# A hybrid streaming encoder layer: first projection in the order value, query, key, value, with queries and keys turned by VectorE

## The chip, the cores and the metric

The kernel runs on one core of one Trainium2 chip. The metric is the device time of one execution in microseconds (us). TensorE (PE) does the matrix products, VectorE (DVE), ScalarE (ACT) and GpSimd (POOL) the rest; SyncE (SP) issues nearly all DMA transfers.

## The reference

One layer of a streaming encoder for 384 tokens: 256 of a new prompt, and 16 for each of 8 running streams. `h` is projected by one matrix into a gated convolution input, queries, keys, values, forget logits and two gates:

```python
h = rmsnorm(x, norm_mix_g)                      # (384, 2048)
proj = h @ w_in                                 # columns: GLU 2048 | q 1024 | k 1024 | v 1024 | f 8 | gates 2 x 2048
q = rmsnorm(q, q_norm_g); k = rmsnorm(k, k_norm_g)          # per head of 128
logf = log_sigmoid(f_logit + b_forget)
b_out = attn_fn(q, k, v, logf) @ w_att_out      # 8 heads, causal, bias from cumsum(logf)
x = x + (gate_a * a_out + gate_b * b_out) @ w_out           # a_out: conv branch
x = x + (silu(gc) * u_half) @ w_down            # ConvGLU feed-forward, width 5632
```

Normalized keys, the values, `logf` and two convolution states are outputs too.

## The kernel before

Everything is float32. Each matrix product is done as three products of rounded halves: a weight pair (256 rows by up to 512 columns) is loaded into a `raw` tile (three buffers), ACT casts it to `hi` (line 145), DVE subtracts to get `lo` (line 146; `hi` and `lo` have three buffers each), and TensorE runs `hi*hi`, `hi*lo` and `lo*hi` for each 128-row tile (lines 239 to 241 where the weights are stationary, 244 to 246 where the activations are). `plan` lists the weight pairs in the order of their use, and `ahead` fetches and splits two or three pairs ahead at a raised priority. `gemm` walks over jobs: 16 row blocks of 128 ("units"), then the eviction of the PSUM tiles; after each unit `tick` advances side work (generators, and functions put off with `after(units, fn)`). TensorE's order is the program's; the orders of DVE, ACT and of the SP queue come from a scheduler that works with those priorities. Each of these queues is in order.

The first stage projects `h` by token rows (three 128-token tiles, so three PSUM tiles a job; five `acc` banks and three `misc` banks rotate):

- values and forget logits in three blocks of 344 columns, `V_COLS`; the first two share a pass over `h`, since in it `x` is still being loaded, turned by TensorE and scaled (`x_chunk`). In the same pass `first_norm` collects the sums of squares; its last steps make the row factor `rs1` (ACT square root, line 111, then DVE), which every eviction of this stage multiplies in (`tok_evac`, lines 426 and 428);
- keys, two blocks of 512, with `bias_rows` at their side, then the key norm on DVE (lines 519 and 520) and the key store;
- queries, two blocks of 512, and the query norm (line 528).

The gated unit follows (four jobs with stationary weights, lines 239 to 241, 16 units each). Beside it runs attention, one head each six units: `head_past_keys`, `head_operands` two units later, `head_scores` two after that. `head_operands` turns the head's queries and keys from token rows to feature rows: three TensorE transposes of `qt` (line 583) and an ACT copy that scales (584), three of `kt` (587) and a DVE copy (588), then a DVE copy of the streams' queries into the padded `qz` (589).

In the mixing stage and the feed-forward the kernel already turns 512-column panels on DVE: `blocks` (line 259) makes 16 block transposes of 32 partitions by 384, of which each turns twelve 32x32 blocks, and puts them where a full transpose would.

Of the kernel before, what the change touches and what calls it, by code (L numbers as in the profile page):

```python
# [15 lines left out]
P = 128  # L16
# [24 lines left out]
def hybrid_step(  # L41
# [31 lines left out]
    def misc_tile():  # L73
        return misc.tile([P, 512], F32, tag="misc", name="misc")
# [97 lines left out]
    FFN_PLAN += [("up", g) for g in range(7, 9)] + [("down", (6, 7))]  # L172
    FFN_PLAN += [("up", g) for g in range(9, 11)] + [("down", (8, 9, 10))]

    planned(w_in, 0, V_COLS[0], 16, V_COLS[1])
    for cols in V_COLS[2:] + K_COLS + Q_COLS + GLU_COLS + GA_COLS + GB_COLS:
        planned(w_in, 0, cols, 16)
    AO_PW = [("ao", 0), ("ao", 1), ("pw", 0), ("ao", 2), ("pw", 1), ("ao", 3), ("pw", 2), ("pw", 3)]
    for what, n in AO_PW:
# [41 lines left out]
    def gemm(jobs, sides=()):  # L221
        for js in jobs:
            js = js if isinstance(js, tuple) else (js,)
            for j in js:
                nb = 4 if j["kind"] == "A" else NTT
                j["ps"] = [(misc_tile if j is not js[0] and i == 2 else acc_tile)() for i in range(nb)]
            for j, k in [(j, k + i) for k in range(0, js[0]["nk"], 2) for j in js for i in range(2)]:
                nb, n, nk, ps = len(j["ps"]), j["n"], j["nk"], j["ps"]
                kk = k % 2
                if kk == 0:  # L230
                    ahead(2 if len(plan) > v_last + 3 else 3)
                    hi, lo = ready.pop(0)
                ah, al = j["act"](k)
                st, sp = k == 0, k == nk - 1
                for m in range(nb):
                    s = slice(m * P, (m + 1) * P)
                    if j["kind"] == "A":
                        o = ps[m][:, :NT]
                        mm(o, hi[:, kk, s], ah, start=st, stop=False)  # L239
                        mm(o, hi[:, kk, s], al, start=False, stop=False)  # L240
                        mm(o, lo[:, kk, s], ah, start=False, stop=sp)  # L241
                    else:
                        o = ps[m][:, :n]
                        mm(o, ah[:, s], hi[:, kk, :n], start=st, stop=False)  # L244
                        mm(o, ah[:, s], lo[:, kk, :n], start=False, stop=False)  # L245
                        mm(o, al[:, s], hi[:, kk, :n], start=False, stop=sp)  # L246
# [141 lines left out]
    def first_norm():  # L388
        for c in range(2, 16, 2):
            if c == 2:  # L390
                yield
            yield
            x_chunk(c)
            yield
            x_chunk(c + 1)
            if c % 4 == 2:
                for t in range(NTT):
                    n = c // 4
                    tc.keep_in_program_order(
                        nc.scalar.activation(junk[:], xs[n][:, t, :], AF.Square, accum_out=ssx[:, t, n:n + 1]))  # L400
# [7 lines left out]
        nc.vector.tensor_copy(rs1[:], r[:])  # L408
# [27 lines left out]

    ha = grouped(hT)
    v_jobs = [job("B", 16, ha, tok_evac(vt, 344 * i, 344, shared=i == 2), n=344) for i in range(3)]
    gemm([(v_jobs[0], v_jobs[1]), v_jobs[2]], [first_norm()])
    close_x0()  # L440


    def tiny(name):
# [21 lines left out]
    nc.sync.dma_start(prompt_v[0, 0].rearrange("(t p) h d -> p t (h d)", p=P), vt[:, 0:2, 0:1024])  # L465
    nc.sync.dma_start(sample_v[0].rearrange("b t h d -> (b t) (h d)"), vt[:, 2, 0:1024])

    p_dr, close_dr = pool("dram", space=bass.MemoryType.DRAM)
    p_b, close_b = pool("bias", side="right")
# [41 lines left out]
        ts(ssf, ssf, 1.0 / P, EPS, op0=ALU.mult, op1=ALU.add)  # L511
        return rsqrt(ssf, [P, NTT * H], p_qkv, f"rq{a}")[:].rearrange("p (t h) -> p t h", t=NTT)

    gemm([job("B", 16, ha, tok_evac(kt, 512 * i, 512, 0)) for i in range(2)], [bias_rows()])
    close_b()
    rk = head_rsqrt(0)
    for t in range(NTT):
        k3 = kt[:, t, :].rearrange("p (h d) -> p h d", h=H)
# [6 lines left out]
    rq = head_rsqrt(1)  # L525
    for t in range(NTT):
        q3 = qt[:, t, :].rearrange("p (h d) -> p h d", h=H)
        tt(q3, q3, rq[:, t, :].unsqueeze(2).to_broadcast([P, H, P]), op=ALU.mult)


    p_att, close_att = pool("att", side="right")
# [42 lines left out]
            load_k(d["h"] + 1)  # L574

    def head_operands(d):
        hs = d["hs"]
        d["vc"], d["bs"] = vbs[d["h"]]
        qT = p_att.tile([P, NT], F32, tag="qT", bufs=2, name="qT")
        kT = p_att.tile([P, NT], F32, tag="kT", bufs=2, name="kT")  # L580
        ps = misc_tile()
        for t in range(NTT):
            tr(ps[:, t * P:(t + 1) * P], qt[:, t, hs], ident[:])
        nc.scalar.activation(qT[:], ps[:, :NT], AF.Identity, scale=qgs[:])
        ps = misc_tile()
        for t in range(NTT):
            tr(ps[:, t * P:(t + 1) * P], kt[:, t, hs], ident[:])
        nc.vector.tensor_copy(kT[:], ps[:, :NT])
        nc.vector.tensor_copy(qz[d["h"] % 2][:, :, :, 0:16], by_stream(qT[:, 2 * P:]))
        d["qT"], d["kT"] = qT, kT  # L590

    def head_scores(d):
        qT, kT, kTs, bs, qzh = d["qT"], d["kT"], d["kTs"], d["bs"], qz[d["h"] % 2]
        s0 = misc_tile()
        mm(s0[:, :P], qT[:, 0:P], kT[:, 0:P], start=True, stop=True)
        s1 = misc_tile()
        mm(s1[:, :2 * P], qT[:, P:2 * P], kT[:, 0:2 * P], start=True, stop=True)
        s2_ = misc_tile()
        mm(s2_[:, P:2 * P], qT[:, 2 * P:], kT[:, 2 * P:], start=True, stop=True)
# [51 lines left out]
    def attention():  # L651
        at = {}
        for d in heads:
            for off, step in ((0, head_past_keys), (2, head_operands), (4, head_scores), (9, head_probs),
                              (11, head_out), (13, head_last)):
# [426 lines left out]
```

## Time and profile before

| | us |
|---|---|
| median of three runs | 2008.67 |
| the runs | 2007.51, 2008.67, 2492.07 |
| the profiled execution | 2007.84 |
| its span in the profile | 2005.8 |

The profile is of one execution. Its page gives the busy time of each engine, the chain of work that ended last, and groups of equal instructions by line; the trace behind it can be asked for who waited for whom and for single instructions. A line such as `60.52 0.32 PE L244 MATMUL acc<-hi,hT ...` gives start and duration in us, engine, source line, operation, the tile written and those read. In brackets stands the idle time of the engine before it and what ended it. The ends of matmuls are modelled and overlap; their starts are what counts.

### The profile page before, as it was taken

What the parts mean: (1) busy time and instruction counts of PE and PEld (TensorE: products, weight loads), DVE (VectorE), ACT (ScalarE), POOL (GpSimd) and SP (SyncE); (2) the same over time, 40 slices, a digit from 0 to 9 for tenths busy, and PEclk for the clock granted to TensorE, in tenths of its full rate; (3) what the DMA queues carried; (4) which work ended last, traced back from release to release, by engine and by line L of the source; (5) the groups of instructions that cost most, each with busy time, mean ns of one, the idle gap of its engine ahead of it and who ended that gap; (6) DMA issues with size and microseconds to landing.
All of it is one profiled execution on the core that took longest, in us unless ns stands there. A gap on an engine that the chain in (4) does not pass through costs nothing.

```text
span 2005.8 us, 24525 instructions
## 1 busy us (share of the span) xinstructions
PE 1995.2 (99%) x9458; PEld 1682.9 (84%) x9458; DVE 1269.1 (63%) x1854; ACT 744.2 (37%) x1085; POOL 87.1 (4%) x214
## 2 busy tenths in 40 slices
PE   9999999999999999999999999999999999999999
PEld 8988999988888888888888888888888888888887
DVE  4434478888765487576767683367673376638663
ACT  5434454433334523333333432233332233323321
POOL 2000001100000000000000010000010000000000
PEclk9999999999999999999999999999999999999999
DMA  6566467444444334534444434444443444344443
GB/s 185 171 176 176 138 155 174 121 134 131 138 130 126 126 124 146 178 124 128 124 131 125 137 122 137 131 127 124 129 137 126 129 124 137 127 127 126 137 156 107
DMA packets 200574, 275.99 MB, mean 138 GB/s; under 512 B 45022, under 2 KB 88049, under 8 KB 200449
## 3 DMA queue, kind: packets, MB, share of 16 engines
q1 hardware_dynamic: 200137, 273.85, 46.0%
q8 instruction: 74, 1.21, 0.2%
q0 software_dynamic: 288, 0.57, 0.2%
q14 instruction: 43, 0.35, 0.1%
q10 hardware_dynamic: 32, 0.01, 0.0%
HBM read 266.98 MB, written 7.86 MB: 137 GB/s over the span
## 4 chain that ended last, share of the span: by engine, by line
PE 95%; DVE 4%; issue 1%; DMA 1%; ACT 0%; SPq 0%; ACTq 0%
PE acc L244 28%; PE acc L246 28%; PE acc L245 28%; PE acc L239 2%; PE acc L240 2%; PE acc L241 2%; DVE mixT L259 1%; DVE lo L146 1%; DMA raw<-in_w_in_dram 1%; DVE sgA L843 0%; DVE uT L259 0%; DVE sgA L844 0%; PE misc L636 0%; PE misc L603 0%; PE misc L285 0%
## 5 line engine op out<-in xcount | busy, mean ns | idle before, releaser
L146 DVE TENSOR_TENSOR lo<-raw,hi 128x1024 fp32r<-128x1024 f32 (+2 forms) x481 | 578.9, 1204 | 592.6 <-ACT hi L145 589.7
L145 ACT CAST hi<-raw 128x1024 fp32r<-128x1024 f32 (+2 forms) x481 | 496.0, 1032 | 1007.0 <-PE acc L246 885.3
L244 PE MATMUL acc<-hi,xg 128*128 128x512 f32 x1056 | 412.3, 390 | 0.0
L246 PE MATMUL acc<-hi,xg 128*128 128x512 f32 x1056 | 411.0, 389 | 0.0
L245 PE MATMUL acc<-lo,xg 128*128 128x512 f32 x1056 | 410.8, 389 | 0.0
L244 PE MATMUL acc<-hi,hT 128*128 128x512 f32 (+1 forms) x704 | 268.0, 381 | 1.9 <-ACT hT L288 1.9
L246 PE MATMUL acc<-hi,hT 128*128 128x512 f32 (+1 forms) x704 | 265.3, 377 | 0.4 <-DVE hT L289 0.4
L245 PE MATMUL acc<-lo,hT 128*128 128x512 f32 (+1 forms) x704 | 265.2, 377 | 0.0
L244 PEld LDWEIGHTS acc<-hi,xg 128*128 128x128 f32 x1056 | 198.2, 188 | 42.0
L246 PEld LDWEIGHTS acc<-hi,xg 128*128 128x128 f32 x1056 | 198.2, 188 | 41.4
L245 PEld LDWEIGHTS acc<-lo,xg 128*128 128x128 f32 x1056 | 198.3, 188 | 40.9
L244 PE MATMUL acc<-hi,act 128*128 128x512 f32 x528 | 205.5, 389 | 0.5 <-DVE y L1027 0.5
L245 PE MATMUL acc<-lo,act 128*128 128x512 f32 x528 | 205.4, 389 | 0.0
L246 PE MATMUL acc<-hi,act 128*128 128x512 f32 x528 | 205.4, 389 | 0.0
L722 DVE SCALAR_TENSOR_TENSOR ut<-ext,cw,ut 128x384 f32<-128x384 f32 x240 | 151.7, 632 | 6.3
L244 PEld LDWEIGHTS acc<-hi,hT 128*128 128x128 f32 x704 | 132.4, 188 | 24.5 <-ACT hT L288 2.1
L246 PEld LDWEIGHTS acc<-hi,hT 128*128 128x128 f32 x704 | 132.3, 188 | 23.2 <-DVE hT L289 0.7
L245 PEld LDWEIGHTS acc<-lo,hT 128*128 128x128 f32 x704 | 132.4, 188 | 22.3
L259 DVE STREAM_TRANSPOSE extf<-tok 32x384 f32<-32x384 f32 x176 | 100.3, 570 | 31.0 <-ACT tok L963 28.2
L259 DVE STREAM_TRANSPOSE uT<-tok 32x384 f32<-32x384 f32 x176 | 100.3, 570 | 29.7 <-ACT tok L963 26.9
L244 PEld LDWEIGHTS acc<-hi,act 128*128 128x128 f32 x528 | 99.1, 188 | 21.5 <-DVE y L1027 0.9
L246 PEld LDWEIGHTS acc<-hi,act 128*128 128x128 f32 x528 | 99.1, 188 | 20.7
(291 smaller groups left out, 2087.4 us busy)
## 6 DMA issues: line engine op xcount, KB each, us to landing
raw<-in_w_up_dram SPq DMA_DIRECT2D x176, 512.0 KB, 3.6
raw<-in_w_in_dram SPq DMA_DIRECT2D x96, 512.0 KB, 3.6
raw<-in_w_down_dram SPq DMA_DIRECT2D x88, 512.0 KB, 3.6
raw<-in_w_in_dram SPq DMA_DIRECT2D x64, 256.0 KB, 3.1
raw<-in_w_out_dram SPq DMA_DIRECT2D x32, 512.0 KB, 3.6
raw<-in_w_att_out_dram SPq DMA_DIRECT2D x16, 512.0 KB, 3.5
raw<-in_conv_pw_out_dram SPq DMA_DIRECT2D x16, 512.0 KB, 3.7
raw<-in_w_in_dram SPq DMA_DIRECT2D x23, 344.0 KB, 3.3
```

The lines of the kernel that those rows point to most:

```text
L145: nc.scalar.copy(hi[:, k, :o], raw[:, k, :o])
L146: tt(lo[:, k, :o], raw[:, k, :o], f(hi[:, k, :o]), op=ALU.subtract)
L239: mm(o, hi[:, kk, s], ah, start=st, stop=False)
L240: mm(o, hi[:, kk, s], al, start=False, stop=False)
L241: mm(o, lo[:, kk, s], ah, start=False, stop=sp)
L244: mm(o, ah[:, s], hi[:, kk, :n], start=st, stop=False)
L245: mm(o, ah[:, s], lo[:, kk, :n], start=False, stop=False)
L246: mm(o, al[:, s], hi[:, kk, :n], start=False, stop=sp)
L259: nc.vector.transpose(put(a, slice(32 * b, 32 * b + 32)), src[32 * a:32 * a + 32, b])
L722: stt(o, v, wc, o, op0=ALU.mult, op1=ALU.add)
```

## The change

- The first stage runs in the order: value blocks 0 and 2 (block 2 holds the forget logits) in one pass, the two query blocks, the two key blocks, value block 1. `plan` follows. The rest of `first_norm` that the first pass doesn't reach, and `bias_rows`, run beside the query blocks, and `x`'s pool is closed after these.
- After the query norm, two panels of queries (four heads each) are turned by `blocks` into `attT`, the tile that later takes the heads' outputs, and scaled in place by ACT. They are put off to units 2 and 12 of the key blocks.
- After the key norm, two panels of keys are turned into the memory of `qt`, put off to units 3 and 13 of the last value block.
- The value store comes after that block, behind the key store.
- `head_operands` has no transposes any more; it does the past keys' step and the copy into `qz`, four units ahead of the scores.

```diff
-    planned(w_in, 0, V_COLS[0], 16, V_COLS[1])
-    for cols in V_COLS[2:] + K_COLS + Q_COLS + GLU_COLS + GA_COLS + GB_COLS:
+    planned(w_in, 0, V_COLS[0], 16, V_COLS[2])
+    for cols in Q_COLS + K_COLS + V_COLS[1:2] + GLU_COLS + GA_COLS + GB_COLS:
...
-    gemm([(v_jobs[0], v_jobs[1]), v_jobs[2]], [first_norm()])
-    close_x0()
+    norm_steps = first_norm()
+    gemm([(v_jobs[0], v_jobs[2])], [norm_steps])
...
-    gemm([job("B", 16, ha, tok_evac(kt, 512 * i, 512, 0)) for i in range(2)], [bias_rows()])
+    gemm([job("B", 16, ha, tok_evac(qt, 512 * i, 512, 1)) for i in range(2)], [norm_steps, bias_rows()])
+    drain(norm_steps)
     close_b()
+    close_x0()
+    rq = head_rsqrt(1)
...
+    def q_panel(n):
+        blocks(qt[:, :, 512 * n:512 * (n + 1)], by_feature(attT[:, 4 * n:4 * n + 4]))
+        for h in range(4 * n, 4 * n + 4):
+            nc.scalar.activation(attT[:, h], attT[:, h], AF.Identity, scale=qgs[:])
+
+    kT = qt[:].rearrange("p t n -> p (t n)").rearrange("p (h x) -> p h x", h=H)
+
+    def k_panel(n):
+        blocks(kt[:, :, 512 * n:512 * (n + 1)], by_feature(kT[:, 4 * n:4 * n + 4]))
+
+    for n in range(2):
+        after(2 + 10 * n, lambda n=n: q_panel(n))
+    gemm([job("B", 16, ha, tok_evac(kt, 512 * i, 512, 0)) for i in range(2)])
     rk = head_rsqrt(0)
...
-    gemm([job("B", 16, ha, tok_evac(qt, 512 * i, 512, 1)) for i in range(2)])
...
+    for n in range(2):
+        after(3 + 10 * n, lambda n=n: k_panel(n))
+    gemm([v_jobs[1]])
+    nc.sync.dma_start(prompt_v[0, 0].rearrange("(t p) h d -> p t (h d)", p=P), vt[:, 0:2, 0:1024])
+    nc.sync.dma_start(sample_v[0].rearrange("b t h d -> (b t) (h d)"), vt[:, 2, 0:1024])
...
     def head_operands(d):
-        hs = d["hs"]
+        head_past_keys(d)
         d["vc"], d["bs"] = vbs[d["h"]]
-        qT = p_att.tile([P, NT], F32, tag="qT", bufs=2, name="qT")
-        kT = p_att.tile([P, NT], F32, tag="kT", bufs=2, name="kT")
-        ps = misc_tile()
-        for t in range(NTT):
-            tr(ps[:, t * P:(t + 1) * P], qt[:, t, hs], ident[:])
-        nc.scalar.activation(qT[:], ps[:, :NT], AF.Identity, scale=qgs[:])
-        ps = misc_tile()
-        for t in range(NTT):
-            tr(ps[:, t * P:(t + 1) * P], kt[:, t, hs], ident[:])
-        nc.vector.tensor_copy(kT[:], ps[:, :NT])
-        nc.vector.tensor_copy(qz[d["h"] % 2][:, :, :, 0:16], by_stream(qT[:, 2 * P:]))
-        d["qT"], d["kT"] = qT, kT
+        nc.vector.tensor_copy(qz[d["h"] % 2][:, :, :, 0:16], by_stream(attT[:, d["h"], 2 * P:]))
```

More of the change, by code (lines that the diff above doesn't have):

```diff
@@ L463, in hybrid_step @@
     nc.sync.dma_start(sample_logf[0].rearrange("b t h -> (b t) h"), lg[:, 2, :])
-    nc.sync.dma_start(prompt_v[0, 0].rearrange("(t p) h d -> p t (h d)", p=P), vt[:, 0:2, 0:1024])
-    nc.sync.dma_start(sample_v[0].rearrange("b t h d -> (b t) (h d)"), vt[:, 2, 0:1024])
     p_dr, close_dr = pool("dram", space=bass.MemoryType.DRAM)
@@ L512, in head_rsqrt @@
         return rsqrt(ssf, [P, NTT * H], p_qkv, f"rq{a}")[:].rearrange("p (t h) -> p t h", t=NTT)
-    gemm([job("B", 16, ha, tok_evac(kt, 512 * i, 512, 0)) for i in range(2)], [bias_rows()])
+    gemm([job("B", 16, ha, tok_evac(qt, 512 * i, 512, 1)) for i in range(2)], [norm_steps, bias_rows()])
+    drain(norm_steps)
     close_b()
+    close_x0()
+    rq = head_rsqrt(1)
+    for t in range(NTT):
+        q3 = qt[:, t, :].rearrange("p (h d) -> p h d", h=H)
+        tt(q3, q3, rq[:, t, :].unsqueeze(2).to_broadcast([P, H, P]), op=ALU.mult)
+    def q_panel(n):
[8 more added lines that the diff above has]
+    gemm([job("B", 16, ha, tok_evac(kt, 512 * i, 512, 0)) for i in range(2)])
     rk = head_rsqrt(0)
@@ L576, in head_operands @@
     def head_operands(d):
-        hs = d["hs"]
+        head_past_keys(d)
         d["vc"], d["bs"] = vbs[d["h"]]
-        qT = p_att.tile([P, NT], F32, tag="qT", bufs=2, name="qT")
-        kT = p_att.tile([P, NT], F32, tag="kT", bufs=2, name="kT")
-        ps = misc_tile()
-        for t in range(NTT):
-            tr(ps[:, t * P:(t + 1) * P], qt[:, t, hs], ident[:])
-        nc.scalar.activation(qT[:], ps[:, :NT], AF.Identity, scale=qgs[:])
-        ps = misc_tile()
-        for t in range(NTT):
-            tr(ps[:, t * P:(t + 1) * P], kt[:, t, hs], ident[:])
-        nc.vector.tensor_copy(kT[:], ps[:, :NT])
-        nc.vector.tensor_copy(qz[d["h"] % 2][:, :, :, 0:16], by_stream(qT[:, 2 * P:]))
-        d["qT"], d["kT"] = qT, kT
+        nc.vector.tensor_copy(qz[d["h"] % 2][:, :, :, 0:16], by_stream(attT[:, d["h"], 2 * P:]))
     def head_scores(d):
-        qT, kT, kTs, bs, qzh = d["qT"], d["kT"], d["kTs"], d["bs"], qz[d["h"] % 2]
+        qh, kh, kTs, bs, qzh = attT[:, d["h"]], kT[:, d["h"]], d["kTs"], d["bs"], qz[d["h"] % 2]
         s0 = misc_tile()
-        mm(s0[:, :P], qT[:, 0:P], kT[:, 0:P], start=True, stop=True)
+        mm(s0[:, :P], qh[:, 0:P], kh[:, 0:P], start=True, stop=True)
         s1 = misc_tile()
-        mm(s1[:, :2 * P], qT[:, P:2 * P], kT[:, 0:2 * P], start=True, stop=True)
+        mm(s1[:, :2 * P], qh[:, P:2 * P], kh[:, 0:2 * P], start=True, stop=True)
         s2_ = misc_tile()
-        mm(s2_[:, P:2 * P], qT[:, 2 * P:], kT[:, 2 * P:], start=True, stop=True)
+        mm(s2_[:, P:2 * P], qh[:, 2 * P:], kh[:, 2 * P:], start=True, stop=True)
         for r in range(2):
@@ L653, in attention @@
         for d in heads:
-            for off, step in ((0, head_past_keys), (2, head_operands), (4, head_scores), (9, head_probs),
+            for off, step in ((0, head_operands), (4, head_scores), (9, head_probs),
                               (11, head_out), (13, head_last)):
```

3 lines of the change are left out of this document (removed).

## The prediction

> **What bounds the kernel now.** I read the page first (busy shares, then the chain that ended last), then TensorE's own waits, then stretches of the first 380 us, then single instructions.
>
> ```profile
> span 2005.8 us, 24525 instructions
> PE 1995.2 (99%) x9458; PEld 1682.9 (84%) x9458; DVE 1269.1 (63%) x1854; ACT 744.2 (37%) x1085; POOL 87.1 (4%) x214
> PE 95%; DVE 4%; issue 1%; DMA 1%; ACT 0%; SPq 0%; ACTq 0%
> PE misc L308 <- POOL ident masks.py:199: 2.5, 1, 2.5
> PE acc L244 <- ACT hT L288: 1.9, 1, 1.9
> PE acc L244 <- DVE y L1027: 0.5, 1, 0.5
> 60.50:83.40 22.90, 22.90 (x150) 22.88 (x149) 8.37 (x13) 8.94 (x15) 0.00 (x0) 1.00 0.59 164
> 83.40:216.70 133.30, 133.30 (x593) 109.69 (x593) 55.60 (x72) 53.39 (x123) 2.31 (x4) 1.00 0.63 176
> 216.70:380.00 163.30, 163.03 (x1191) 156.44 (x1190) 123.50 (x274) 83.00 (x176) 15.46 (x25) 1.00 0.60 151
> ```
>
> TensorE is busy for 99% of the span and its longest waits are 2.5, 1.9 and 0.5 us. Of the three stretches (last value block; keys and queries; gated unit with attention; the columns are length, then busy time of PE, PEld, DVE, ACT and POOL) TensorE has no idle time in the first two and 0.27 us in the third. So every TensorE instruction taken out shortens the program, and every wait put in front of TensorE lengthens it; DVE (55.6 of 133.3 us in the key and query stretch) and ACT have room as long as nobody waits for them. The profiled execution took 2007.84 us, its span and 2.0 us around it. The runs shown are 2007.51, 2008.67 and one far-off 2492.07, so their median 2008.67 is 0.8 above the execution I reckon from.
>
> **The saving: 48 TensorE transposes.** Per head six go (three of queries, three of keys).
>
> ```profile
> L583 PE MATMUL misc<-ident,qt 128*128 128x128 f32 x24 | 3.9, 272 | 0.0
> 233.04 0.33 PE L240 MATMUL acc<-hT,hi 128*128 128x384 f32 x1
> 233.21 0.34 PE L241 MATMUL acc<-hT,lo 128*128 128x384 f32 x1
> 233.39 0.49 PE L583 MATMUL misc<-ident,qt 128*128 128x128 f32 x3
> 233.71 0.49 PE L587 MATMUL misc<-ident,kt 128*128 128x128 f32 x3
> 233.96 0.42 PE L239 MATMUL acc<-hT,hi 128*128 128x384 f32 x1
> 234.22 0.33 PE L240 MATMUL acc<-hT,hi 128*128 128x384 f32 x1
> 234.39 0.34 PE L241 MATMUL acc<-hT,lo 128*128 128x384 f32 x1
> ```
>
> Durations overlap (each matmul starts about 0.17 us after the one before, although it lasts 0.33), so I count starts. Without the transposes the matmul of 233.96 would start at 233.39 (0.57 us), and the one after it follows by 0.26 instead of 0.17 (0.09 us). That is 0.66 us a head, 8 x 0.66 = 5.3 us in all. The ends are 8 x 0.57 = 4.6, and the summed durations, 48 x 0.272 = 13.1. I take 5.3, because the starts are what the next matmul sees. The page "TensorE: Matmul & The Clock Gate" of the Trainium skill, Part 4 (PE-mode transpose), gives about 275 ns for a 128x128 transpose inside a kernel (measured there on bf16). The 272 ns of the row agree with that as a duration; by that price the saving would be 48 x 0.275 = 13.2 us, and the start times say that it isn't the price in a full pipeline.
>
> DVE also loses eight copies out of PSUM and gains 64 block transposes; ACT's eight scalings of queries stay, only moved to the key stage. The rest of TensorE's work is the same: the blocks change their order, not their widths.
>
> **The reordered start: a wait at the first block's end.** The first block still pairs two 344-wide value blocks, but it is now followed by a 512-wide query block instead of the last value block.
>
> ```profile
> 55.48 0.75 ACT L145 CAST hi<-raw 128x688 fp32r<-128x688 f32 x1
> 56.87 1.28 ACT L111 ACT_TABLE_LOAD   x1
> 58.17 0.20 ACT L111 ACTIVATE r1s<-mt 128x3 f32<-128x3 f32 x1
> 58.28 0.75 ACT L145 CAST hi<-raw 128x688 fp32r<-128x688 f32 x1
> 59.61 0.55 ACT L428 ACTIVATE vt<-acc,rs 128x344 f32<-128x344 f32 x1 [0.58 <-DVE rs L408]
> 57.68 0.32 PE L244 MATMUL acc<-hi,hT 128*128 128x344 f32 x1
> 60.37 0.32 PE L246 MATMUL misc<-hi,hT 128*128 128x344 f32 x1
> 60.52 0.32 PE L244 MATMUL acc<-hi,hT 128*128 128x344 f32 x1
> ```
>
> The paired block ends at 60.52, where the next block needs the PSUM bank of the first value tile. Now the norm's square root runs at 58.17, its factor reaches the first eviction at 59.61, and that eviction ends at 60.16: only 0.4 us before it is needed. In the changed kernel's issue order on ACT a second weight cast stands ahead of the square root, and a third ahead of the evictions. A cast needs a free hi tile, and there are three, so that second cast waits for the weight pair that TensorE finishes at 57.68 (the matmul there opens the last pair of 18). With about 0.2 us of signalling and a cast of 1.0 us the table load starts at 58.85, the square root at 60.15, and the factor is there at 61.6 (1.44 us later, as now from 58.17 to 59.61). The third cast needs the block's end, 60.5, and runs to 61.7; then the eviction, to 62.3. TensorE can start the query block at 62.3 instead of 60.5: a new wait of 1.8 us. Its bounds are 0 (if the order were no obstacle, as now) and 2.7 (if the third cast starts only when the factor is there: 61.6 + 1.05 + 0.55 - 60.5). I take 1.8, by the rows.
>
> The other moves at this place cost nothing: the log-gate arithmetic and the convolution weights' transposes keep their distance to the work that reads them, and the cover is DVE's 14.5 idle us of 22.9 in the first stretch above. If that cover were gone, the six matmuls of the bias rows would wait, no others. The transfers that grow from 344 to 512 KB in this place fall into a stretch with a DMA share of 0.59.
>
> **Query panels during the first key block.** 32 block transposes go in here.
>
> ```profile
> 711.65 3.48 DVE L259 STREAM_TRANSPOSE mixT<-sgA 32x384 f32<-32x384 f32 x6
> 715.16 1.23 DVE L146 TENSOR_TENSOR lo<-raw,hi 128x1024 fp32r<-128x1024 f32 x1
> 157.12 1.22 DVE L146 TENSOR_TENSOR lo<-raw,hi 128x1024 fp32r<-128x1024 f32 x1 [0.76 <-ACT hi L145]
> 159.86 2.36 DVE L519 TENSOR_TENSOR kt<-kt,rq0r 128x1024 f32<-128x1024 f32 x2
> 159.80 1.05 ACT L145 CAST hi<-raw 128x1024 fp32r<-128x1024 f32 x1 [1.18 <-PE acc L246]
> 163.88 1.05 ACT L145 CAST hi<-raw 128x1024 fp32r<-128x1024 f32 x1 [3.02 <-PE acc L246]
> 150.28 0.69 ACT L428 ACTIVATE kt<-acc,rs 128x512 f32<-128x512 f32 x1 [1.67 <-PE acc L246]
> 150.96 0.75 DVE L426 TENSOR_SCALAR kt<-acc,rs 128x512 f32<-128x512 f32 x1 [1.10 <-PE acc L246]
> 151.44 0.39 PE L244 MATMUL acc<-hi,hT 128*128 128x512 f32 x1
> 151.00 0.31 ACT L433 ACTIVATE jk<-kt 128x128 f32<-128x128 f32 x1
> 153.36 0.67 ACT L428 ACTIVATE kt<-acc,rs 128x512 f32<-128x512 f32 x1
> ```
>
> The same kind of transpose in the mixing stage runs six in 3.48 us with no gap to the next piece: 0.585 us each. So the panels bring 64 x 0.585 = 37.4 us to DVE, half of it here. TensorE takes a weight pair each 4.08 us (casts at 159.80 and 163.88), and DVE owes it one lo piece (1.23 us) in that time. A lo piece can be late: after its cast TensorE still has two pairs to do, 8.16 - 0.2 - 1.05 - 1.23 = 5.7 us.
>
> I lay the changed issue order of DVE on the clock of the present key-to-query change, which has the same steps. The query norm (three multiplications) starts at 159.86; lo pieces are then due at 160.85, 164.9, 169.0, 173.1, 177.2 and 181.3, and the order puts 0, 2, 6, 7, 6 and 6 transposes ahead of them. They start at 162.1, 165.8, 170.5, 175.9, 180.6 and 185.4: late by up to 4.1, inside the 5.7. Then stand three more transposes, and behind them DVE's eviction of the first key block, at 188.4 instead of 183.6 (32.64 us, eight pairs, after the 150.96 of the row). ACT's squares of that tile wait for it, and behind them on ACT stand the third eviction (0.67) and the cast of a weight pair, which so ends at 192.0 instead of 185.3. Its lo piece ends at 193.3, and TensorE wants it at 151.44 + 32.64 + 8.16 = 192.2 (at 151.44 the present key block has ended and the next one begins). A wait of 1.1 us. At the 570 ns of the rows' mean it is 0.7; if the casts slip into gaps, 0. The upper end is below, with the slower rival.
>
> **Key panels during the last value block.** The same count, with a pair of 18 x 0.158 = 2.84 us (60.52 less 57.68), then the gated unit's 4.18. The same walk gives the value block's pieces at least 2.6 us before they are needed, and the first pieces of the gated unit 2.3, 1.2 and 0.6 us before: I take 0, with 1.5 as upper end. SP's queue is moved too. The store of the keys stands ahead of the second weight load of the gated unit and waits for the key norm, some 2.4 us (its last two multiplications, 2.36 in the row of 159.86); but the lo piece of that load stands behind seven transposes on DVE, and these end later than the load arrives. Both stores, 3.1 MB, now fall into about 23 us beside 2.9 MB of weights; if the 204 GB/s of the first 40 us were the most that can be had,
>
> ```profile
> 0.00:40.00 40.00, 35.23 (x217) 34.30 (x218) 15.95 (x25) 20.36 (x38) 10.54 (x32) 1.00 0.71 204
> ```
>
> the last byte comes 6 us late, about the slack of the loads (5.7): 0 to 1 us, and I take 0, for the DMA share was only 0.71 there. In attention the queries and keys lie ready long before the scores of unit 9, so nothing is added, and ACT and DVE have less to do.
>
> **Sum.** 2007.84 - 5.3 + 1.8 + 1.1 = 2005.4 us.
>
> **Rivals.**
> (a) The waits hide: casts and evictions come through as now, for TensorE has no wait at any present block change in the rows above. 2007.84 - 5.3 = 2002.5. Against it stands the 0.4 us of margin at 60.16.
> (b) DVE becomes the bound, and the change makes the kernel slower. The page "VectorE: DVE Perf Modes" of the Trainium skill, under its rules for kernel authors, says to use TensorE for a 128x128 transpose when PSUM will do as its destination; that speaks against this change, and in DVE time the rows agree (37.4 us gained for 4.4 of copies).
>
> ```profile
> 708.09 0.54 issue
> 708.63 0.57 DVE mixT L259
> L588 DVE COPY kT<-misc 128x384 f32<-128x384 f32 x8 | 4.4, 552 | 10.1 <-PE misc L587 10.1
> ```
>
> The chain shows a piece of 0.54 marked "issue" in the mixing stage, one for every four transposes. Were it real time, a transpose would cost 0.57 + 0.14 = 0.72 instead of 0.585. Then the 30 ahead of the eviction put it 4 us later: 4.6 us of waiting there rather than 1.1, plus 3 in the gated unit, 2005.4 + 3.5 + 3 = 2011.9. It decides against the change from about 0.66 us a transpose, where the waits eat 5.3. The six in 3.48 us speak against it.
> (c) The saving does not arrive, because TensorE in the gated unit is paced by something else (DVE is busy 123.5 of 163.3 us there): 2007.84 + 1.8 + 1.1 = 2010.7. Against it stand 0.27 us of TensorE idle in that stretch.
> (d) The transposes cost their full 272 ns: 2007.84 - 13.1 + 2.9 = 1997.6, against the start times.
>
> **How the numbers follow.** Forecast 0.62, (a) 0.17, (b) 0.11, (c) 0.08, (d) 0.02. The time is the forecast's 2005.4; its own range, from the bounds of the waits (0 to 2.7, 0 to 2, 0 to 1.5) is 2003.5 to 2008. The range of 8 in 10 takes in (a) and the scatter of about 1 us of the runs: 2001.5 to 2009.0. A change of over 2%, about what a measurement of this kernel can tell from no change, would be 40 us. No case comes near, so within 2% has 0.98.
>
> **What would show it.** 9410 matmuls instead of 9458 and no transposes of queries or keys by TensorE; a TensorE wait of about 1.8 us near 60 to 62 us, released by an eviction of the value tile; one of about 1 us at the second key block, released by a lo piece; DVE's block transposes at 0.585 us each. The forecast is wrong if the first wait is missing or over 3 us, if lo pieces are missed several times while a panel is in work, or if the gated unit does not get about 5 us shorter.

## The result, and the profile after

The changed kernel takes 2010.53 us (median of 22 runs, 2006.19 to 2013.18) against 2008.47 for the kernel before, run beside it: ratio 1.0012, 95% interval 1.0006 to 1.0017. The forecast was 2005.4 us, within 2001.5 to 2009.0. The profiled execution took 2010.66 us, with a span of 2008.6, 2.8 more than before. First the page's head and chain, then TensorE's waits (total, times, longest), then three stretches: the 22.9 us behind the paired block (now the start of the queries), all from 83.4 us to the gated unit, and the whole gated unit (length, busy time of PE, PEld, DVE, ACT, POOL, then granted clock, DMA share, GB/s).

```profile
span 2008.6 us, 24491 instructions
PE 1993.7 (99%) x9410; PEld 1679.5 (84%) x9410; DVE 1302.0 (65%) x1910; ACT 743.9 (37%) x1085; POOL 88.0 (4%) x214
PE 90%; DVE 6%; issue 1%; ACT 1%; DMA 1%; SPq 0%; DVEq 0%; ACTq 0%
```

```profile
PE misc L308 <- POOL ident masks.py:199: 2.5, 1, 2.5
PE acc L244 <- DVE vt L426: 1.8, 1, 1.8
PE misc L637 <- DVE mx L614: 1.7, 1, 1.7
PE acc L244 <- ACT hT L288: 1.6, 1, 1.6
PE acc L245 <- DVE lo L146: 0.7, 1, 0.7
```

```profile
62.50:85.40 22.90, 22.88 (x97) 18.06 (x98) 10.74 (x31) 8.01 (x13) 0.00 (x0) 0.93 0.39 112
83.40:220.80 137.40, 136.67 (x654) 116.25 (x653) 78.19 (x103) 59.06 (x154) 3.33 (x4) 1.00 0.56 156
220.80:391.50 170.70, 168.52 (x1194) 161.27 (x1194) 138.82 (x295) 79.65 (x151) 15.82 (x25) 0.99 0.62 162
```

The 48 matmuls are gone (9410), yet TensorE's busy time fell by only 1.5 us, DVE's share of the chain rose from 4 to 6%, and three waits stand where there was none: 1.8 and 0.7 us, both forecast, and 1.7 us on line 637, which wasn't. In two of the stretches the granted clock is below 1.00.

Where the 2.8 us came from is read from the first and last start of line 239, which brackets the gated unit; the first row is of the kernel before, the second of the changed one.

```profile
L239 PE MATMUL acc<-hT,hi x256: 333/334/443, 216.7 to 388.9; 128*128 128x384 f32 x128
```

```profile
L239 PE MATMUL acc<-hT,hi x256: 333/334/667, 220.8 to 391.5; 128*128 128x384 f32 x128
```

The gated unit starts 4.1 us later, lasts 170.7 instead of 172.2 us (forecast: 166.9), and what follows it is 0.2 us longer: 4.1 - 1.5 + 0.2 = 2.8.

**The first 4.1 us.** ScalarE's, VectorE's and TensorE's rows of the changed kernel at the end of the paired block:

```profile
57.92 1.05 ACT L145 CAST hi<-raw 128x1024 fp32r<-128x1024 f32 x1 [0.76 <-PE acc L246]
58.99 1.28 ACT L111 ACT_TABLE_LOAD   x1
60.28 0.20 ACT L111 ACTIVATE r1s<-mt 128x3 f32<-128x3 f32 x1
60.76 1.04 ACT L145 CAST hi<-raw 128x1024 fp32r<-128x1024 f32 x1 [0.28 <-PE misc L246]
61.73 1.86 ACT L428 ACTIVATE vt<-acc,rs 128x344 f32<-128x344 f32 x4
```

```profile
61.52 0.17 DVE L408 COPY rs<-r1r 128x3 f32<-128x3 f32 x1
61.80 0.57 DVE L426 TENSOR_SCALAR vt<-acc,rs 128x344 f32<-128x344 f32 x1
```

```profile
62.52 0.47 PE L244 MATMUL acc<-hi,hT 128*128 128x512 f32 x1 [1.79 <-DVE vt L426]
...
65.23 0.63 PE L246 MATMUL acc<-hi,hT 128*128 128x512 f32 x1
65.66 0.63 PE L244 MATMUL acc<-hi,hT 128*128 128x512 f32 x1
```

```profile
63.40:67.00 3.60, 3.60 (x11) 2.78 (x10) 2.41 (x12) 2.13 (x4) 0.00 (x0) 0.53 0.48 146
```

The wait is the forecast one: cast, table load, square root, factor, eviction. The third cast of the forecast ends at 61.80, but the factor (line 408) is not written before 61.69 either, so that cast adds next to nothing; the eviction that the profile names as the releaser is VectorE's. But behind the wait the matmuls follow each other in 0.43 us instead of 0.23 (65.23 to 65.66): for 3.6 us the granted clock is 0.53, which costs 3.6 x 0.47 = 1.7 us that no wait shows. Such a stretch is called a spell below.

The other forecast wait, on a lo piece at the second key block, came by the forecast chain too. VectorE's eviction of the first key block stands behind three more query transposes, ScalarE's cast behind that eviction, and TensorE waits for the lo piece:

```profile
167.59 1.74 DVE L259 STREAM_TRANSPOSE attT<-qt 32x384 f32<-32x384 f32 x3
169.37 0.75 DVE L426 TENSOR_SCALAR kt<-acc,rs 128x512 f32<-128x512 f32 x1
171.97 1.03 ACT L145 CAST hi<-raw 128x1024 fp32r<-128x1024 f32 x1
174.32 0.50 PE L245 MATMUL acc<-lo,hT 128*128 128x512 f32 x1 [0.73 <-DVE lo L146]
```

Together 1.8 + 1.7 + 0.7 = 4.2, against 4.1 measured.

**The gated unit.** Its wait comes late, before the output of the sixth head. TensorE, then a stretch behind it, then DVE:

```profile
346.28 0.49 PE L637 MATMUL misc<-vt,pT 128*128 128x128 f32 x2 [1.74 <-DVE mx L614]
```

```profile
346.30:350.00 3.70, 3.70 (x27) 3.18 (x28) 2.17 (x12) 3.31 (x9) 0.00 (x0) 0.56 1.13 273
```

```profile
334.19 3.02 DVE L727 SCALAR_TENSOR_TENSOR ut<-ext,cw,ut 128x384 f32<-128x384 f32 x4
337.13 1.23 DVE L587 STREAM_TRANSPOSE kTs<-kc 128x1024 f32<-128x1024 f32 x1
...
339.63 1.22 DVE L146 TENSOR_TENSOR lo<-raw,hi 128x1024 fp32r<-128x1024 f32 x1
340.77 0.61 DVE L727 SCALAR_TENSOR_TENSOR ut<-ext,cw,ut 128x384 f32<-128x384 f32 x1
341.30 1.22 DVE L146 TENSOR_TENSOR lo<-raw,hi 128x1024 fp32r<-128x1024 f32 x1
342.43 1.92 DVE L727 SCALAR_TENSOR_TENSOR ut<-ext,cw,ut 128x384 f32<-128x384 f32 x3
344.27 1.22 DVE L146 TENSOR_TENSOR lo<-raw,hi 128x1024 fp32r<-128x1024 f32 x1
345.40 0.61 DVE L727 SCALAR_TENSOR_TENSOR ut<-ext,cw,ut 128x384 f32<-128x384 f32 x1
345.93 0.28 DVE L614 CUSTOM_DVE_ANT_0 pr<-misc,bs 128x128 f32<-128x128 f32 x1
```

TensorE had finished the seventh head's scores at 342.2, and wants one of their three PSUM banks at 344.54. The reduction that frees the bank (line 614) stands on DVE behind a run of convolution taps (line 727) and three lo pieces, and starts at 345.93. In the kernel before the same reduction stands ahead of the last lo piece:

```profile
340.17 1.92 DVE L722 SCALAR_TENSOR_TENSOR ut<-ext,cw,ut 128x384 f32<-128x384 f32 x3
342.01 0.28 DVE L609 CUSTOM_DVE_ANT_0 pr<-misc,bs 128x128 f32<-128x128 f32 x1
...
342.56 1.22 DVE L146 TENSOR_TENSOR lo<-raw,hi 128x1024 fp32r<-128x1024 f32 x1
```

Over the whole gated unit both kernels run 78 of these taps. But in the 17 us that end some 5 us ahead of this place (322.8 to 339.8; in the kernel before 318.7 to 335.7, as far from the gated unit's start) the changed kernel runs 19 of them, 12.1 us, and the kernel before 14, 8.9 us: they come in another order.

Again the clock falls behind the wait: 3.7 us at 0.56, 3.7 x 0.44 = 1.6 us. 172.2 - 5.3 + 1.7 + 1.6 = 170.2, against 170.7 measured. The panels themselves did what was forecast: in the group below each transpose takes 570 ns by the mean of the rows, and six in a row take 3.48 us (162.83 to 166.31), as in the mixing stage. Of the 32 transposes of the key panels, however, only six run beside the value block; the other 26 (14.5 us) fall into the first 21 us of the gated unit.

```profile
L259 DVE STREAM_TRANSPOSE attT<-qt 32x384 f32<-32x384 f32 x32 | 18.2, 570 | 0.6
```

### The profile page after: what moved, and what is told of

It reads as the page before. It is cut to its first block, busy times and chain, and to the rows that moved or that the text cites. A ratio compares the mean times of both kernels' runs of the same rounds, so it can differ in the third digit from the quotient of the medians.

```text
span 2008.6 us, 24491 instructions
## 1 busy us (share of the span) xinstructions
PE 1993.7 (99%) x9410; PEld 1679.5 (84%) x9410; DVE 1302.0 (65%) x1910; ACT 743.9 (37%) x1085; POOL 88.0 (4%) x214
## 4 chain that ended last, share of the span: by engine, by line
PE 90%; DVE 6%; issue 1%; ACT 1%; DMA 1%; SPq 0%; DVEq 0%; ACTq 0%
PE acc L244 27%; PE acc L246 27%; PE acc L245 27%; PE acc L239 2%; PE acc L241 2%; PE acc L240 2%; DVE lo L146 2%; DVE mixT L259 1%; DMA raw<-in_w_in_dram 1%; DVE attT L259 1%; ACT jk L433 0%; DVE sgA L848 0%; DVE uT L259 0%; ACT hi L145 0%; DVE sgA L849 0%
```

## The experiments

The theory: the transposes do save 5.3 us, and the loss is two waits that come from the order of work on ScalarE and VectorE, each with a spell of some 3.6 us at about half clock behind it. Rivals: the saving is smaller; moving transposes to VectorE loses by itself; VectorE has no room in the gated unit. All times are medians of 11 runs, with the kernel before run beside them.

| kernel | us | before | ratio, 95% interval | gated unit, us | wait near 60 us | waits on DVE in the gated unit |
|---|---|---|---|---|---|---|
| changed kernel (22 runs) | 2010.53 | 2008.47 | 1.0012 (1.0006 to 1.0017) | 170.7 | 1.8 | 1.7 |
| 1 order only | 2011.96 | 2009.01 | 1.0011 (1.0002 to 1.0019) | 172.1 | 1.8 | none |
| 2 keys only | 2005.80 | 2009.01 | 0.9987 (0.9978 to 0.9996) | 169.4 | none | none |
| 3 root first | 2007.87 | 2008.72 | 0.9995 (0.9986 to 1.0004) | 170.3 | none | 1.7 |
| 4 wait filled | 2008.62 | 2008.72 | 1.0001 (0.9992 to 1.0009) | 169.1 | filled | 1.7 |
| 5 cast first | 2011.48 | 2008.72 | 1.0009 (1.0000 to 1.0018) | 170.7 | 1.8 | 1.7 |
| 6 root and cast first | 2007.11 | 2008.72 | 0.9993 (0.9985 to 1.0002) | 171.0 | none | 1.7 |
| 7 copies on ScalarE | 2009.76 | 2009.01 | 1.0003 (0.9994 to 1.0012) | 170.1 | 1.8 | 1.6 |
| 8 lo pieces first | 2012.00 | 2009.01 | 1.0016 (1.0007 to 1.0025) | 171.3 | 1.8 | 2.6, 0.8, 0.2 |
| 9 casts and lo pieces first | 2010.47 | 2009.19 | 1.0010 (1.0001 to 1.0018) | 170.7 | 1.8 | 1.3, 1.1, 2 x 0.2 |
| 10 scores first | 2008.23 | 2009.19 | 0.9996 (0.9987 to 1.0005) | 168.0 | 1.8 | 1.2 |
| 11 root and scores first | 2004.90 | 2009.19 | 0.9980 (0.9971 to 0.9989) | 168.8 | none | 1.2 |
| 12 past keys too | 2009.09 | 2009.29 | 1.0001 (0.9992 to 1.0010) | 172.3 | none | 2.4 and 0.7 |

"Gated unit" is the first to last start of its first matmul line. The 0.27 us wait before a transpose of the convolution input, which every kernel here and the one before has, is left out, and so is one of up to 0.5 us for ScalarE's eviction of the last value block, which some of the kernels have.

### Each half of the change alone

**1. The new block order alone**, with the heads of the kernel before:

```diff
-        head_past_keys(d)
+        hs = d["hs"]
...
+            tr(ps[:, t * P:(t + 1) * P], qt[:, t, hs], ident[:])
...
+            tr(ps[:, t * P:(t + 1) * P], kt[:, t, hs], ident[:])
```

> The changed block order alone: value blocks 0 and 2, queries, keys, value block 1, but queries and keys stay in token rows and TensorE turns them for each head as in the kernel before (48 transposes back, no panels on VectorE). Theory (the order costs a 1.8 us wait at the first block's end and a stretch at half clock behind it, and the transposes on VectorE give a net gain of about 1 us in the gated unit): the wait near 60 us is there with a low granted clock in 60 to 70 us in most executions, no wait on a lo piece at the second key block, the gated unit is as long as before (172 us from first to last matmul of line 239), and the time is 2 to 4 us over the kernel before, 2010.5 to 2012.5, so at or above that of the changed kernel. Rival (the order is free and the loss comes from VectorE's transposes): no wait near 60 us, time within 0.7 us of the kernel before, 2008 to 2009.5.

Measured 2011.96 us (before: 2009.01). The wait near 60 us is there, released by the same eviction; no wait on a lo piece; the gated unit 172.1 us, as before:

```profile
PE acc L244 <- DVE vt L426: 1.8, 1, 1.8
```

```profile
60.00:70.00 10.00, 8.21 (x30) 6.41 (x29) 5.72 (x21) 5.96 (x10) 0.00 (x0) 0.83 0.40 121
```

The order costs 2 to 3 us by itself (by the ratio and by the medians); the rows show 1.8 us of wait and, at 0.83 over 10 us, 1.7 us of clock. The rival that it is free falls.

**2. Only the keys on VectorE**, in the order of before: 24 transposes fewer on TensorE, 32 more on DVE during the query blocks.

```diff
+    def k_panel(n):
+        blocks(kt[:, :, 512 * n:512 * (n + 1)], by_feature(attT[:, 4 * n:4 * n + 4]))
...
-        for t in range(NTT):
-            tr(ps[:, t * P:(t + 1) * P], kt[:, t, hs], ident[:])
-        nc.vector.tensor_copy(kT[:], ps[:, :NT])
```

> The order of before; only the keys are turned by VectorE, as panels during the query blocks, and the queries by TensorE for each head: 24 transposes fewer. Theory (transposes on VectorE save TensorE 0.33 us a head and the loss sits in the order of the first stage and in VectorE's own order in the gated unit): no wait at 60 us, full clock there, 9434 matmuls, gated unit 169.5 to 171 us if no wait behind a reduction of scores comes up, 2.6 us less than before in all: 2005.5 to 2007 by the result. If VectorE's order at the fifth and sixth head brings the wait of 1.7 us (line 614) here too: 2007.5 to 2009. Rival (moving transposes to VectorE loses by itself, through lo pieces that come late in the panel stretch): waits on lo pieces of 1 us and more, 2009 or above.

Measured 2005.80 us, 3.2 below the kernel before. The gated unit is 2.8 us shorter, where counting starts gives 24 x 0.66 / 6 = 2.6; its one new wait is 0.5 us on a lo piece in the first stage, and no wait behind a reduction of scores came up. So turning panels on VectorE does not lose by itself, and the price per transpose was right.

### The wait near 60 us, and the clock behind it

**3. The square root ahead of the second weight cast** on ScalarE, and the third cast behind the last eviction: an order on the queue alone, with no wait added (`NoSync`).

```diff
+        if gate:
+            tc.add_manual_dep(d.ins, gate.pop().ins.name, mybir.DependencyInfo(
+                mybir.DependencyClass.NoSync, mybir.DependencyReason.DATA), reason="order")
```

> The changed kernel with two orderings on ACT at the end of the first paired block: the second weight cast stands behind the norm's square root, and the third behind the evictions. Theory (clock windows and ACT order): the TensorE wait of 1.8 us at 60 us goes, and with it the half-clock window behind it (3.5 us at 0.53, some 1.6 us); TensorE's first wait in that place is under 0.4 us, the granted clock of 60 to 70 us is 1.00, the gated unit starts 3.4 us earlier (217.4 instead of 220.8). The wait in the gated unit (1.7 us) and its half-clock window stay. Span near 2005.2, about 3.4 under the changed kernel. Rival (DVE capacity: DVE paces the gated unit, and what TensorE wins ahead of it is given back there): the gated unit starts 3.4 us earlier too but gets longer by as much; span near 2008.

Measured 2007.87 us (before: 2008.72). No wait and full clock in this stretch (rows of 60 to 70 us, here and next):

```profile
60.00:70.00 10.00, 10.00 (x50) 8.50 (x49) 8.52 (x29) 6.76 (x11) 0.00 (x0) 1.00 0.53 157
```

By the ratios (0.9995 for 1.0012) it gains 3.4 us on the changed kernel, twice the wait. In the traced execution the gated unit starts only 2.2 us earlier, at 218.6 and not at the 217.4 that was expected: TensorE's wait for `hT` near 16 us, which the kernel before has too (1.9 us there), was 2.3 us here, and a spell followed it (granted clock 0.84 from 10 to 20 us).

**4. The wait filled with work.** Seven matmuls into a spare PSUM tile, whose result nobody reads, stand where TensorE waited. The queries start as long after the block's end as without them, 1.95 us; only the idleness is gone.

```diff
+    fill = misc_tile()
+    for _ in range(FILL_END):
+        mm(fill[:, :P], ident[:], ident[:], start=True, stop=True)
```

> The changed kernel with seven idle matmuls (identity by identity, about 1.5 us, results not used) behind the first paired block, where TensorE waits 1.8 us. Theory (an idle stretch makes the clock fall): the query block still starts at about 62.5 us, but the granted clock of 60 to 70 us is 1.00 instead of 0.83, so the gated unit starts some 1.6 us earlier (about 219.2). Rival (the clock falls for another reason, such as the start of the 512-wide matmuls): the clock stays at 0.83 there and nothing is won.

Measured 2008.62 us, and full clock, with 0.23 us of idleness left:

```profile
60.00:70.00 10.00, 9.77 (x56) 8.58 (x55) 6.90 (x24) 7.93 (x12) 0.00 (x0) 1.00 0.55 158
```

1.0001 for 1.0012 is 2.2 us gained though no data come earlier; the two intervals overlap a little, so the size rests more on the rows. They separate the two parts of the loss: the wait's length stays, and the clock's part goes: from the first matmul of the queries to the gated unit it is 156.7 us instead of 158.3. The expected start of the gated unit, 219.2, was missed all the same (220.9): in this execution, too, a spell followed the wait near 16 us (2.2 us; granted clock 0.90 and 0.93 in the two stretches from 10 to 30 us), and everything behind it is that much later. This execution also kept its full clock behind the 1.7 us wait in the gated unit, which lasted 169.1 us instead of 170.7 with the same wait: 1.6 us once more.

### The wait in the gated unit

**5. The newest weight cast ahead of the copy of the turned probabilities** on ScalarE, and **6. the same with the root first.**

```diff
+        cast[0] = nc.scalar.copy(hi[:, k, :o], raw[:, k, :o])
...
+        tc.add_manual_dep(d_pT.ins, cast[0].ins.name, mybir.DependencyInfo(
+            mybir.DependencyClass.NoSync, mybir.DependencyReason.DATA), reason="order")
```

> The changed kernel with one ordering on ACT: the copy of the transposed probabilities stands behind the newest weight cast. By the issue order this moves one cast at heads 5 and 6 ahead of that copy, and nothing else there. Theory (ACT order): the cast at about 339 us goes at about 335.8, the wait of 1.7 us at 344.5 and the half-clock window behind it go, the gated unit takes about 167.4 us instead of 170.7, span near 2005.3. Rival (DVE capacity): DVE was busy without a gap from 325 to 345 us, so the scores' reduction comes as late as before, the wait stays at 1.5 us or more, and the gated unit still takes 170 us or more.

> The orderings of e1 and e5 together in the changed kernel. Theory: both waits and both half-clock windows go: span near 2001.8, 4 us under the kernel before (ratio 0.998), and granted clock 1.000 over the span. Rival (DVE capacity): the gated unit keeps its wait or gets another one, span 2005 or more.

Measured 2011.48 and 2007.11 us. In 5 a cast now stands ahead of the copy (338.35 and 341.04 us), as meant, but the wait of 1.7 us stays in both: this order on ScalarE is not its cause. With the root first, 6 does no better than 3 (0.9993 and 0.9995).

**7. Three small copies of each head moved from VectorE to ScalarE** (lines 643, 648, 654).

```diff
-        nc.vector.tensor_copy(on[:], pn[:, :P])
+        nc.scalar.copy(on[:], pn[:, :P])
```

> The changed kernel with three small copies of each head (the probabilities' output and the two copies into the head outputs) moved from VectorE to ScalarE: about 1 us less for VectorE in each head's 16.5 us, its order otherwise nearly the same. Theory (order of VectorE): the 1.7 us wait behind line 614 stays above 1 us, gated unit 170 to 171 us, 2009.5 to 2011. Rival (VectorE's load, 16.5 us of work in a period of 16.5 us): the wait shrinks below 0.7 us and no low clock follows, gated unit 167 to 169 us, 2007 to 2008.5.

Measured 2009.76 us. VectorE is busy for 133.2 us of the gated unit instead of 138.8, 0.7 us less in each head, and the wait is 1.6 us: a load smaller by that much does not remove it.

**8. Taps and the transposes of past keys behind the newest lo piece** on VectorE, and **9. this together with 5.**

```diff
-                stt(o, v, wc, o, op0=ALU.mult, op1=ALU.add)
+                behind_lo(stt(o, v, wc, o, op0=ALU.mult, op1=ALU.add))
```

> The changed kernel, and on VectorE every convolution tap and every transpose of past keys in the gated unit stands behind the newest lo piece issued, so that no run of taps can put itself ahead of one. Theory (VectorE's order: a run of taps ahead of a lo piece pushes the scores' reduction of head six back by some 2 us): the 1.7 us wait behind line 614 and the low clock after it go, gated unit 167 to 169 us, time 2 to 3.5 us under the changed kernel, 2007 to 2008.5. Rival (VectorE has no room left in this stretch, so any order leaves a wait somewhere): the wait stays or moves to another instruction, 170 us or more, 2009.5 to 2011.

> The changed kernel with both orders at once: on ScalarE the copy of the turned probabilities stands behind the newest weight cast, and on VectorE the taps and the transposes of past keys stand behind the newest lo piece. Each alone left the wait: with the first the lo piece still stood behind taps, with the second the cast stood behind the copy. Theory (each of two queues holds the weight split back, and both have to be mended): casts and lo pieces come one in about 4.2 us through heads five and six, the wait behind line 614 falls below 0.5 us, gated unit 167 to 169 us, 2007 to 2009. Rival (no room on VectorE): waits of more than 1 us somewhere in the gated unit, 170 us or more, 2009.5 to 2012.

Measured 2012.00 and 2010.47 us: by the ratios (1.0016 and 1.0010) neither differs from the changed kernel (1.0012). In 8 the wait is longer, 2.6 us, in 9 shorter, 1.3. The theory that late lo pieces alone are the fault falls. In 8 VectorE now idles for up to 3.85 us in one piece, and the lo pieces still bunch, three within 5.6 us ahead of the reduction (the rows are of experiment 8, whose line numbers there are six higher):

```profile
PE misc L643 <- DVE mx L620: 3.4, 2, 2.6
```

```profile
335.88 0.29 DVE L660 COPY attT<-misc 128x128 f32<-128x128 f32 x1 [3.85 <-PE misc L659]
...
342.07 1.23 DVE L148 TENSOR_TENSOR lo<-raw,hi 128x1024 fp32r<-128x1024 f32 x1 [1.16 <-ACT hi L147]
...
343.75 1.22 DVE L148 TENSOR_TENSOR lo<-raw,hi 128x1024 fp32r<-128x1024 f32 x1
...
346.47 1.22 DVE L148 TENSOR_TENSOR lo<-raw,hi 128x1024 fp32r<-128x1024 f32 x1
...
348.66 0.28 DVE L620 CUSTOM_DVE_ANT_0 pr<-misc,bs 128x128 f32<-128x128 f32 x1
```

**10. The taps behind the newest reduction of scores** (lines 614 and 727 of the changed kernel).

```diff
+            last_red[0] = nc.vector.tensor_tensor_reduce(out=v, in0=sp_[:, :n * P], in1=bs[:, o * P:(o + n) * P], scale=1.0,
...
+                behind_scores(stt(o, v, wc, o, op0=ALU.mult, op1=ALU.add))
```

> The changed kernel; on VectorE the convolution taps of the gated unit stand behind the newest reduction of scores issued before them (line 614), which removes the five taps that stood between three lo pieces and that reduction at head six. Theory (order of VectorE: with the taps behind it the reduction ends about 2 us earlier than TensorE needs the bank): the 1.7 us wait and the low clock near 346 us go, gated unit 167 to 169 us, time 1.5 to 3.5 us under the changed kernel, 2007 to 2009. Rival (pieces of weights, not taps, hold the reduction, or VectorE has no room): the wait stays above 1 us or moves, gated unit 170 us or more, 2009.5 to 2011.5.

Measured 2008.23 us, 1.0012 down to 0.9996 (3.2 us). The reduction starts at 342.44 instead of 345.93, and the wait at this place is gone:

```profile
341.29 1.22 DVE L146 TENSOR_TENSOR lo<-raw,hi 128x1024 fp32r<-128x1024 f32 x1 [0.34 <-ACT hi L145]
342.44 0.28 DVE L621 CUSTOM_DVE_ANT_0 pr<-misc,bs 128x128 f32<-128x128 f32 x1
```

```profile
PE misc L615 <- DVE kTs L587: 1.2, 1, 1.2
```

```profile
220.80:388.80 168.00, 166.54 (x1194) 159.92 (x1194) 129.78 (x283) 78.54 (x148) 16.09 (x22) 1.00 0.63 164
```

A smaller wait came up at the eighth head, on a transpose of past keys. 168.0 less this 1.2 is 166.8 us at full clock: the 166.9 that the prediction's saving gives. The rule does more than change places around this reduction: 12 of the 78 taps move behind the gated unit, so VectorE has 10 us less to do in it. That taps ahead of the reduction made the wait is shown; order and load aren't wholly separated by it.

**11. Root first and scores first together** (3 and 10).

> The changed kernel with the square root of the norm ahead of the second weight cast on ScalarE (no wait at the first block's end) and the taps behind the scores' reduction on VectorE (no wait in the gated unit). Theory (the loss consists of these two waits and the low clock behind each): neither wait, full clock in 60 to 70 us and in the gated unit, gated unit 167 to 169 us, about 5 us under the changed kernel: 2003.5 to 2005.5, 3 to 5 us under the kernel before. Rival (the saving of 48 transposes is not 5.3 us): 2006 to 2008 although both waits are gone.

Measured 2004.90 us (2003.52 to 2006.61), ratio 0.9980 (0.9971 to 0.9989): 4.3 us below the kernel before, and by the medians 5.6 below the changed one. Neither of the two waits is there (the 1.2 us of experiment 10 is, and 0.5 us for ScalarE's eviction of the last value block), and the stretch from 60 to 70 us has its full clock:

```profile
span 2002.3 us, 24490 instructions
```

```profile
60.00:70.00 10.00, 10.00 (x45) 8.26 (x45) 7.45 (x25) 6.02 (x9) 0.00 (x0) 1.00 0.50 147
```

**12. The taps also behind the newest transpose of past keys**, to take away the last 1.2 us.

```diff
-        nc.vector.transpose(kTs[:].rearrange("p b k -> p (b k)"), kcs[d["h"]][:])
+        last_red[0] = nc.vector.transpose(kTs[:].rearrange("p b k -> p (b k)"), kcs[d["h"]][:])
```

> As the kernel with the root ahead and the taps behind the scores' reductions, and the taps also behind the newest transpose of past keys. That kernel still had a wait of 1.2 us in the gated unit, released by such a transpose, which stood behind taps. Theory (the transpose of past keys comes late only because taps stand ahead of it on VectorE): that wait falls below 0.3 us, gated unit 167 to 168 us, 2003 to 2004.5. Rival (VectorE is full, one wait only takes the place of another): a wait of about 1 us at another instruction of the gated unit, 168.5 us or more, 2004.5 to 2006.5.

Measured 2009.09 us; that wait went, and two others came, the larger one a head later than in the changed kernel:

```profile
359.88 0.49 PE L652 MATMUL misc<-vt,pT 128*128 128x128 f32 x2 [2.36 <-DVE mx L629]
```

So the rival's kind of outcome is what was measured, and more of it, for the time lies above the ranges of both: one more rule for the order moved the wait and did not remove it. That VectorE is full isn't shown by it (it idles 3.85 us in one piece here too). Why the scheduler's order bunches the pieces at these heads stays open.

## Why the prediction was wrong, point by point

- **The saving of 5.3 us held.** Key transposes alone gave 2.8 for 2.6 (2), and the gated unit without its large wait comes to 166.8 for 166.9 us (10). The 48 x 0.272 = 13.1 us of summed durations, and the 275 ns each of the Trainium skill ("TensorE: Matmul & The Clock Gate", Part 4) are not what it costs in a full pipeline.
- **The wait at the first block's end held** (1.8 forecast, 1.79 measured, by the forecast chain), and so did **the wait on a lo piece** (0.7 for 1.1). That 0.7 is also what the prediction names for transposes of 570 ns is chance: the eviction came 4.8 us late, as forecast with 0.585 (at 169.37; eight pairs, 32.64 us, after the one at 131.91 would be 164.55). What differs is that a pair's first matmul needs only `hi`: it started at 173.19, and the one behind it waited. For the key panels and both stores 0 was taken, with 1.5 as bound; 0.17 us shows, for ScalarE's eviction of the last value block behind a cast that had waited for its weights.
- **The step that failed first** is "In attention the queries and keys lie ready long before the scores of unit 9, so nothing is added, and ACT and DVE have less to do." For ScalarE that is so (79.7 us busy for 85.3), for VectorE it isn't (138.8 for 132.1, because of the 26 key transposes), and neither says who waits. The scheduler ordered VectorE's queue anew, and there a reduction that frees a PSUM bank came to stand behind taps and lo pieces: 1.7 us (10). The late key transposes end near 242 us, 100 us ahead of this wait, and VectorE idles in between, so they don't hold the reduction directly. Rival (c), at 2010.7, had the time nearly right by luck: it has the saving not arrive, and the saving did arrive; a smaller load did not remove the wait (7), and moving the taps did (10).
- **The step that failed second** is the sum itself, which prices a wait at its length. Behind both new waits the granted clock fell, 1.7 and 1.6 us. 2007.84 - 5.3 + 1.8 + 0.7 = 2005.0; with 1.7 for the wait in the gated unit and 1.7 + 1.6 for the clock it is 2010.0, of 2010.66 measured. Most of the 0.6 left comes from how a wait is counted: idle time begins at the modelled end of the matmul before, and by starts, as the transposes were counted, the three waits cost 0.5 us more (62.52 instead of about 60.57, 174.32 for 173.42, 346.28 for 344.37).
- The range ended at 2009.0, because no bound had a price for the clock. It also started from 2007.84, an execution at a mean clock of 1.000; the medians of the kernel before lie 0.6 to 1.5 us higher, and 74 of its 108 executions beside the experiments have a lower mean clock.
- Smaller slips changed nothing in the forecast: 0.57 + 0.14 is 0.71, 1.1 + 4 is 5.1 and not 4.6, so rival (b) comes to 2012.4, and the bounds 0 to 2.7, 0 to 2 and 0 to 1.5 span 2002.5 to 2008.7. Nor is 2% the least that can be told apart: the intervals here reach 0.0005 to 0.001 to each side.

**What the clock does to the runs.** Each execution's mean granted clock shows roughly how many such spells it had: one of 3.6 us at 0.53 takes 0.0008 of the mean. Medians in us, with the number of runs (of the kernel before its 108 beside the experiments):

| mean clock | before | changed | root and scores first |
|---|---|---|---|
| 1.000 | 2007.3 (34) | 2006.2 (1) | 2004.5 (7) |
| 0.999 | 2009.2 (70) | 2008.7 (3) | 2006.4 (4) |
| 0.998 | 2010.7 (4) | 2010.4 (12) | |
| 0.997 | | 2012.2 (6) | |

Each step down is about 1.8 us. At equal clock the changed kernel is a little faster than the one before (0.3 to 1.1 us, from few runs in some cells); it loses because it mostly has two or three spells where the other has none or one. The third comes from the wait near 16 us, as old as the kernel before: in the traces a spell followed it in five (experiments 3, 4, 5, 8 and 9, where it was 2.2 to 2.8 us) and in none of the nine others (0.8 to 1.9 us). That the one spell of the kernel before is this one fits, but its only trace has none. The kernel of experiment 11 mostly has none.

## What to carry to other kernels

Price a new TensorE wait of about 1.6 us or more at its length plus a half-clock spell (here some 1.7 us, in most executions), and where it can't be removed, work without use in its place can win the second part back. Work taken off one engine lets a scheduler reorder the others' queues: follow the instruction that frees a PSUM bank in the new order, not only the busy shares. Of a change with two parts, try each alone; here the key panels in the old order were worth 2.6 to 3.2 us, and the new order cost 2 to 3.

## What the runs showed of the hardware

- Waits of 1.6 to 1.8 us were enough for some 3.6 us at a granted clock of 0.53 to 0.56. At the two places of this change 11 of 13 such waits in the traces brought it. The others passed at 1.00: the 1.7 us in the gated unit in experiment 4, and the 1.8 us near 62 us in experiment 9. So did the 2.6 us in the gated unit in experiment 8, the 1.9 us near 16 us of the kernel before, and all waits of 1.1 to 1.3 us (experiments 9 to 11). The Trainium skill, "TensorE: Matmul & The Clock Gate", Part 1, describes a free-running window of about 3.4 us. The length of the spells agrees with that, and so does it that the same wait sometimes passes; but the same page's advice, under "Why this matters for your kernels", to have no gaps of over about 3 us lets these waits through, and here the measurement decides. What decides in a single execution was not tried.
- A 128x128 transpose on TensorE takes 0.11 us of a full pipeline (0.66 us for six), though its row shows 272 ns.
